# Splitting a whole 128x2048 weight unit per instruction in the expert stage, with three persistent places

## The chip, the cores and the metric

One Trainium2 chip, of which one core runs. The metric is device microseconds of one execution. Engines: TensorE (PE, with PEld for its weight loads), VectorE (DVE), ScalarE (ACT), GpSimd (POOL) and SyncE (SP), which issues the loads from HBM.

## The reference, cut to what matters

Three blocks on 256 tokens of width 1024: a hybrid layer, a retention block and a Fourier block with a mixture of experts. The change acts in the last part:

```
for e in range(N_EXPERTS):                       # 8 experts, top-k gates
    out = out + gates[:, e:e+1] * swiglu(t, w_gate[e], w_up[e], w_down[e])
```

where swiglu is (silu(t @ w_gate) * (t @ w_up)) @ w_down. Everything is float32.

## The kernel before, in words

All weights come as 475 **units** of 128x2048 float32 (1 MB). `fetch` (L101) starts one DMA on SP into a raw buffer; the raw buffers come from pools that grow as earlier tensors are released (6, then 4, 2 and 2 more), and a buffer that held an activation (xT) is used as one more in the experts, 15 in all there. A program-order list `raw` holds what has been fetched.

A float32 product is built from three fast products. `split` (L117) takes one **half** of the oldest raw unit, 128x1024: ScalarE copies it with rounding to wh (L128), VectorE writes the rest, raw - wh, to wl (L129). Both lie in a pool of WB = 4 halves. `half` (L171) issues the next split ahead and hands out the oldest split half. TensorE multiplies the activations' high part by wh, their low part by wh, and their high part by wl. So a split may write a place only when TensorE has read the half that was there, four halves earlier.

The experts start near 895 us: 8 experts of 42 units. An expert is 7 strips s = 0..6. A strip has 6 units, here called **G1, G2** (gate), **U1, U2** (up) and **D1, D2** (down, of strip s-1). The order is written out by hand for TensorE and SP only: G1, turn(s-1), G2, U1, U2, D1, D2. `turn` transposes h of the strip before (L1194 or L1196); ScalarE and VectorE then make hx from it (L1200, L1201), which the down units read. After the gate units ScalarE makes sg (L1177), after the up units VectorE makes h from the product and sg (L1184). The order on ScalarE and VectorE is set by a scheduler.

An expert with at most 64 tokens runs U and D **packed** (`either`): two matmuls (L1139, L1144) per piece in place of three (L1142, L1143, L1144), that is 8 matmuls per unit and not 12. Gate units always take 12. By their matmuls, experts 0, 2, 3, 4 are packed and 1, 5, 6, 7 are not. At an expert's end come y (L1232), at the start of the next one the sums into acc (L1254).

Of the kernel before, what the change touches and what calls it, by code (L numbers as in the profile page):

```python
# [9 lines left out]
F32 = mybir.dt.float32  # L10
F32R = mybir.dt.float32r
I32 = mybir.dt.int32
AF = mybir.ActivationFunctionType
ALU = mybir.AluOpType
AX = mybir.AxisListType

P = 128
# [5 lines left out]
E = 8  # L23
FE = 3584
NFE = FE // P
UN = 2048
UE = 42
# [36 lines left out]
def kernel(  # L64
# [10 lines left out]
    nc = tc.nc  # L75
    NU = ws_d.shape[0]
    WB = 4
    HP = 300
    HQ = 512
    HU = UN // 2  # L80

    NRAW, R2N, R3N, R4N = 6, 4, 2, 2
    const = ctx.enter_context(tc.tile_pool(name="const", bufs=1))
    rawp = ctx.enter_context(tc.tile_pool(name="rawp", bufs=NRAW))
    wp = ctx.enter_context(tc.tile_pool(name="wp", bufs=WB))
    psp = ctx.enter_context(tc.tile_pool(name="psp", bufs=2, space=bass.MemoryType.PSUM))
    ctx.enter_context(tc.manual_schedule(engines={mybir.EngineType.PE, mybir.EngineType.SP}))

# [1 line left out]
    raw = []  # L90
    wq = []
    nf = [0]

    def fetch(pool):

        if nf[0] < NU:
            t = pool if isinstance(pool, bass.AP) else pool.tile([P, UN], F32, tag="raw", name="raw")

            edges = {0: (0, HQ, HU, UN), NU - 1: (0, HU, UN)}.get(nf[0], (0, UN))
            for a, b in zip(edges, edges[1:]):  # L100
                nc.sync.dma_start(t[:, a:b], ws_d[nf[0]][:, a:b])  # L101
                if nf[0] == 0 and a < HU:
                    for k in (0,) if a == 0 else range(2, KD, 2):
                        nc.sync.dma_start(xT[:, k:k + 2], xT_d[:, k:k + 2])
            raw.append((t, pool))
            nf[0] += 1
        elif isinstance(pool, bass.AP):
            nc.sync.dma_start(pool[:, 0:D], fnorm_d)

    def more_room(name, n):  # L110
        pool = ctx.enter_context(tc.tile_pool(name=name, bufs=n))
        for _ in range(n):
            fetch(pool)

    half_ = [0, 0]

    def split(scales=None, between=None):  # L117


        if not raw or (half_[1] == H_F2 and scales is None):  # L120
            return
        half_[1] += 1
        r = raw[0][0][:, half_[0] * HU:(half_[0] + 1) * HU]
        wh = wp.tile([P, HU], F32R, tag="wh", name="wh")
        wl = wp.tile([P, HU], F32R, tag="wl", name="wl")
        if scales is None:
            for o in (slice(0, HQ), slice(HQ, HU)) if half_[1] == 1 else (slice(0, HU),):
                nc.scalar.activation(out=wh[:, o], in_=r[:, o], func=AF.Copy)  # L128
                nc.vector.tensor_tensor(out=wl[:, o], in0=r[:, o], in1=wh[:, o].bitcast(F32), op=ALU.subtract)  # L129
                if between is not None and o.start == 0:  # L130
                    between()
        else:
            for t in range(2):
                o = slice(t * 512, t * 512 + 512)
                nc.scalar.activation(out=wh[:, o], in_=r[:, o], func=AF.Copy, scale=scales[:, t:t + 1])
                nc.vector.scalar_tensor_tensor(out=wl[:, o], in0=r[:, o], scalar=scales[:, t:t + 1],
                                               in1=wh[:, o].bitcast(F32), op0=ALU.mult, op1=ALU.subtract)
        wq.append((wh, wl))
        if half_[0]:
            fetch(raw.pop(0)[1])  # L140
        half_[0] ^= 1
# [8 lines left out]
    def advance(item):  # L150
        try:
            item[0] = next(item[1]) or 1
        except StopIteration:
            side.remove(item)
# [16 lines left out]
    def half(ahead=True):  # L171

        for item in list(side):
            item[0] -= 1
            if item[0] <= 0:
                advance(item)
        if ahead:
            split()
        return wq.pop(0)

    def bank(tag="mm", shape=(P, 2, S)):
        return psp.tile(list(shape), F32, tag=tag, name=tag, bufs={"mm": 4, "sd": 2, "dn": 2}[tag])
# [3 lines left out]
    def mm3T(ps, u, b, xh, xl, start, stop):  # L186
        wh, wl = u
        c = slice(b * P, (b + 1) * P)
        mm(ps, wh[:, c], xh, start=start, stop=False)  # L189
        mm(ps, wh[:, c], xl, start=False, stop=False)  # L190
        mm(ps, wl[:, c], xh, start=False, stop=stop)  # L191
# [10 lines left out]
    def unit_late(xh, xl, late=2):  # L202

        ps = [bank("mm", (P, S)) for _ in range(2)]
        us = []
        for cb in range(2):
            us.append(half())
            for k in range(KD - late):
                mm3T(ps[cb], us[cb], k, xh[:, k], xl[:, k], k == 0, False)
        for cb in range(2):  # L210
            for k in range(KD - late, KD):
                mm3T(ps[cb], us[cb], k, xh[:, k], xl[:, k], False, k == KD - 1)
        return ps

    def stripX(xh, xl, mid=None):
# [51 lines left out]
    def col(c, n=1):  # L267
        return cols[:, c:c + n]
# [104 lines left out]
    with pa:  # L373
# [9 lines left out]
        def hilo(dst, j, src):  # L383
# [11 lines left out]
                                in1=col(C_N1, 8).unsqueeze(2).to_broadcast([P, KD, 4]), op=ALU.mult)  # L395
# [342 lines left out]
    with ExitStack() as pr:  # L738
# [120 lines left out]
        for c in range(KD):  # L859
            ps = bank("mm", (P, S))  # L860
            for j in range(16):
                if j % 8 == 0:
# [16 lines left out]
                            in1=col(C_FFN1, 8).unsqueeze(2).to_broadcast([P, KD, E]), op=ALU.mult)  # L879
# [4 lines left out]
    with ExitStack() as pn:  # L884
# [113 lines left out]
        with tc.high_priority(HP):  # L998
            for t in range(2):
# [3 lines left out]
                                    in1=L.unsqueeze(3).to_broadcast([P, 2, E, E]), op=ALU.subtract)  # L1003
# [7 lines left out]
        for c in range(0, KD, 2):  # L1011
            ps, o = to_tok(xT_, c, "mm")
# [8 lines left out]
        with tc.high_priority(HP):  # L1021
            nc.vector.scalar_tensor_tensor(out=pos.rearrange("p a b -> p (a b)"),
                                           in0=ps[:, 0:2].rearrange("p a b -> p (a b)"),
# [35 lines left out]


    pt.close()
    if R4N:
        more_room("raw4p", R4N)
    xT_flat = xT.rearrange("p a b -> p (a b)")
    fetch(xT_flat)
    fn = xT_flat[:, 0:D]
    with ExitStack() as pe:
# [214 lines left out]
        r = Q.tile([P, 2], F32, name="fr")  # L1282
# [12 lines left out]
        def out_rms():  # L1295
            nc.vector.tensor_tensor(out=v, in0=v4[:, :, 0], in1=v4[:, :, 1], op=ALU.add)
            rsqrt(r, v, 2, 1.0 / D)
# [6 lines left out]
        with tc.tile_pool(name="O", bufs=1) as O:  # L1304
            ecur = O.tile([P, E], F32, name="ecur")
            emask = O.tile([P, E], F32, name="emask")
            epos = O.tile([P, 2], F32, name="epos")
            egts = O.tile([P, 2], F32, name="egts")
            etmp = O.tile([P, 2, E], F32, name="etmp")
            with tc.If(n_over[0] + n_over[1] > 0):  # L1310

                nc.vector.tensor_copy(out=ecur, in_=io8)
                with tc.For_i(0, E, 1) as ev:
                    nc.vector.tensor_scalar(out=emask, in0=ecur, scalar1=-8.0, scalar2=None, op0=ALU.is_equal)
                    for src, dst in ((pos, epos), (gts, egts)):
                        nc.vector.tensor_tensor(out=etmp, in0=src, in1=emask.unsqueeze(1).to_broadcast([P, 2, E]), op=ALU.mult)
                        nc.vector.tensor_reduce(out=dst, in_=etmp, axis=AX.X, op=ALU.add)
                    nc.vector.tensor_scalar(out=epos, in0=epos, scalar1=float(-P), scalar2=None, op0=ALU.add)
                    cnt_ = [0]
                    cur_ = []  # L1320

                    def ohalf(ahead=True):
                        i, h = divmod(cnt_[0], 2)
                        if h == 0:
                            t = rawp.tile([P, UN], F32, tag="raw", name="oraw")
                            nc.sync.dma_start(t, ws_d[bass.ds(ev * UE + (NU - E * UE + i), 1)].rearrange("a p n -> p (a n)"))
                            cur_[:] = [t]
                        r = cur_[0][:, h * HU:(h + 1) * HU]
                        wh = wp.tile([P, HU], F32R, tag="wh", name="owh")
                        wl = wp.tile([P, HU], F32R, tag="wl", name="owl")  # L1330
                        nc.scalar.activation(out=wh, in_=r, func=AF.Copy)
                        nc.vector.tensor_tensor(out=wl, in0=r, in1=wh.bitcast(F32), op=ALU.subtract)
                        cnt_[0] += 1
                        return wh, wl

                    oex, osot, ors, steps = gather(lambda t: epos[:, t:t + 1], lambda t: epos[:, t:t + 1])
                    for f in steps:
                        f()
                    combine(experts(oex, ors, ohalf), osot, lambda t: egts[:, t:t + 1])
                    nc.vector.tensor_scalar(out=ecur, in0=ecur, scalar1=-1.0, scalar2=None, op0=ALU.add)  # L1340
                for hf in range(2):
                    out_sumsq(hf)
                out_rms()

        for hf in range(2):
            o = slice(hf * 512, hf * 512 + 512)
# [169 lines left out]
```

## Time and profile before

| what | us |
|---|---|
| runs: 1871.48, 1874.96, 1871.95; median | 1871.95 |
| the profiled execution, its own time | 1872.74 |
| its span | 1871.0 |
| PE busy | 1817.4 (97%) |
| DVE busy | 1482.0 (79%) |
| ACT busy | 1210.6 (65%) |
| L129 (wl), 906 instructions | 1078.5 |
| L128 (wh), 906 instructions | 922.0 |

The busy shares are averages over stages with different limits. In the expert stage VectorE is much busier than over the whole span, so the stage is read by windows and by its own rows.

### The profile page before, as it was taken

How to read it: one execution, taken by the hardware profiler on the slowest of the kernel's cores; microseconds unless marked ns; L12 is line 12 of the kernel's file. 1: busy time of each engine (PE TensorE's matmuls, PEld its weight loads, DVE VectorE, ACT ScalarE, POOL GpSimd, SP SyncE). 2: the span in 40 equal slices, each digit the busy share in tenths (PEclk: the TensorE clock that was granted, in tenths of full speed). 3: DMA queues.
4: the chain of work that ended last, by engine and by line, in shares of the span. 5: the costliest groups of instructions: out<-in, count | busy, mean ns of one | idle time of the engine just before them, and what ended most of it. 6: DMA issues, size and time to landing. Idle time of an engine off the chain costs nothing. (4 is left out here: it accounts for less than half of the span.)

```text
span 1871.0 us, 28740 instructions
## 1 busy us (share of the span) xinstructions
PE 1817.4 (97%) x10890; PEld 1574.5 (84%) x10890; DVE 1482.0 (79%) x1855; ACT 1210.6 (65%) x1484; POOL 158.2 (8%) x154
## 2 busy tenths in 40 slices
PE   8999999999999999999999999999999999999997
PEld 7999999999888999998777887777777788888885
DVE  5666676657677666656899989999999998988987
ACT  5765454455344444446787777888878777777775
POOL 2302122211111122110000000000000000000000
PEclk9999999999999999999999999999999999999999
DMA  8344544555444564544799998999999999999970
GB/s 313 140 154 168 193 178 183 181 181 197 158 150 159 189 248 184 187 170 180 295 419 377 353 367 326 411 386 377 415 354 413 381 353 364 332 356 354 343 290 36
DMA packets 71156, 505.77 MB, mean 270 GB/s; under 512 B 7888, under 2 KB 8016, under 8 KB 10320
## 3 DMA queue, kind: packets, MB, share of 16 engines
q1 hardware_dynamic: 70992, 503.53, 70.7%
q8 instruction: 110, 1.80, 0.4%
q14 instruction: 54, 0.44, 0.1%
HBM read 502.45 MB, written 1.05 MB: 269 GB/s over the span
## 5 line engine op out<-in xcount | busy, mean ns | idle before, releaser
L129 DVE TENSOR_TENSOR wl<-raw,wh 128x1024 fp32r<-128x1024 f32 (+1 forms) x906 | 1078.5, 1227 | 235.3 <-ACT wh L128 226.2
L128 ACT ACTIVATE wh<-raw 128x1024 fp32r<-128x1024 f32 (+1 forms) x906 | 922.0, 1053 | 428.9 <-PE mm L190 188.7
L189 PE MATMUL mm<-xh,wh 128*128 128x256 f32 x1248 | 357.5, 286 | 6.7 <-ACT xh L342 6.7
L1144 PE MATMUL mm<-wl,ex 128*128 128x512 f32 x896 | 356.0, 397 | 3.7 <-DVE wl L129 3.7
L190 PE MATMUL mm<-xl,wh 128*128 128x256 f32 x1248 | 355.2, 285 | 1.0 <-DVE xl L343 0.7
L191 PE MATMUL mm<-xh,wl 128*128 128x256 f32 x1248 | 354.9, 284 | 0.8 <-DVE wl L129 0.8
L1142 PE MATMUL mm<-wh,ex 128*128 128x512 f32 x672 | 270.4, 402 | 0.0
L1143 PE MATMUL mm<-wh,ex 128*128 128x512 f32 x672 | 266.1, 396 | 0.2 <-DVE ex L1103 0.2
L189 PEld LDWEIGHTS mm<-xh,wh 128*128 128x128 f32 x1248 | 237.9, 191 | 8.2 <-ACT xh L342 6.7
L190 PEld LDWEIGHTS mm<-xl,wh 128*128 128x128 f32 x1248 | 237.9, 191 | 2.4 <-DVE xl L343 2.3
L191 PEld LDWEIGHTS mm<-xh,wl 128*128 128x128 f32 x1248 | 237.7, 190 | 1.1 <-DVE wl L129 1.0
L1144 PEld LDWEIGHTS mm<-wl,ex 128*128 128x128 f32 x896 | 168.6, 188 | 54.2 <-DVE wl L129 13.7
L1144 PE MATMUL dn<-wl,hx 128*128 128x512 f32 x448 | 183.6, 410 | 12.1 <-DVE wl L129 11.9
L1143 PEld LDWEIGHTS mm<-wh,ex 128*128 128x128 f32 x672 | 126.7, 189 | 28.2 <-DVE ex L1103 0.5
L1142 PEld LDWEIGHTS mm<-wh,ex 128*128 128x128 f32 x672 | 126.6, 188 | 26.0 <-ACT wh L128 0.3
L1144 PEld LDWEIGHTS dn<-wl,hx 128*128 128x128 f32 x448 | 84.2, 188 | 55.8 <-DVE wl L129 40.1
L190 PE MATMUL mm<-hl,wh 128*128 128x256 f32 x352 | 99.8, 283 | 0.0
L191 PE MATMUL mm<-hh,wl 128*128 128x256 f32 x352 | 99.8, 283 | 0.0
L189 PE MATMUL mm<-hh,wh 128*128 128x256 f32 x352 | 99.8, 283 | 0.0
L1139 PE MATMUL dn<-wh,hx 128*128 128x512 f32 x224 | 89.2, 398 | 0.0
L1142 PE MATMUL dn<-wh,hx 128*128 128x512 f32 x224 | 88.9, 397 | 0.0
L1139 PE MATMUL mm<-wh,ex 128*128 128x512 f32 x224 | 88.7, 396 | 0.0
(400 smaller groups left out, 2500.7 us busy)
## 6 DMA issues: line engine op xcount, KB each, us to landing
raw<-in_ws_dram SPq DMA_DIRECT2D x451, 1024.0 KB, 6.3
xT<-in_ws_dram SPq DMA_DIRECT2D x22, 1024.0 KB, 7.0
raw<-in_ws_dram SPq DMA_DIRECT2D x3, 512.0 KB, 6.3
xT<-in_xT_dram SPq DMA_DIRECT2D x4, 256.0 KB, 5.4
xT<-in_xT_dram SPq DMA_DIRECT2D x1, 1024.0 KB, 8.3
out_dram<-acc SPq DMA_DIRECT2D x4, 256.0 KB, 2.1
cstA<-in_cst_dram SPq DMA_DIRECT2D x1, 576.0 KB, 9.1
raw<-in_ws_dram SPq DMA_DIRECT2D x2, 256.0 KB, 4.5
```

What stands on the lines that cost most here:

```text
L128: nc.scalar.activation(out=wh[:, o], in_=r[:, o], func=AF.Copy)
L129: nc.vector.tensor_tensor(out=wl[:, o], in0=r[:, o], in1=wh[:, o].bitcast(F32), op=ALU.subtract)
L189: mm(ps, wh[:, c], xh, start=start, stop=False)
L190: mm(ps, wh[:, c], xl, start=False, stop=False)
L191: mm(ps, wl[:, c], xh, start=False, stop=stop)
L1139: mm(out_, e, wh, start=first, stop=False)
L1142: mm(out_, e, wh, start=first, stop=False)
L1143: mm(out_, xk[:, P:2 * P], wh, start=False, stop=False)
L1144: mm(out_, e, wl, start=False, stop=last)
```

## The change

From the third expert unit on, one ScalarE and one VectorE instruction split a whole unit, 128x2048, at every second call of `split`. The four half places become two persistent tiles, `ring` (high and low parts, 4 halves each). In the experts the ring is seen as two places of a unit each; a third place, `wp3`, is added for high and low, and stands where two raw buffers (raw4p) were: 13 raw buffers are left in the experts. Units take the three places in turn, so a split waits for TensorE's last read of the unit three before: D1 for G2 of its own strip, D2 for U1, the next G1 for U2. The last unit is still split in halves.

```
-    NRAW, R2N, R3N, R4N = 6, 4, 2, 2
+    NRAW, R2N, R3N = 6, 4, 2
...
-    wp = ctx.enter_context(tc.tile_pool(name="wp", bufs=WB))
+    wp = ctx.enter_context(tc.tile_pool(name="wp", bufs=1))
+
+    ring = [wp.tile([P, WB, HU], F32R, name=f"ring{n}") for n in "hl"]
+    H_MOE = 2 * (NU - E * UE)
+    places = [[r.rearrange("p a n -> p (a n)")[:, i * UN:(i + 1) * UN] for r in ring] for i in (0, 1)]
+    if H_MOE % WB:
+        places.reverse()
...
+        if half_[1] >= H_MOE + WB:
+
+            r, pool = raw[0]
+            wide = half_[1] < 2 * NU - 2
+            if not (wide and half_[0]):
+                wh, wl = places[(half_[1] - H_MOE) // 2 % 3]
+                o = slice(0, UN) if wide else slice(half_[0] * HU, (half_[0] + 1) * HU)
+                nc.scalar.activation(out=wh[:, o], in_=r[:, o], func=AF.Copy)
+                nc.vector.tensor_tensor(out=wl[:, o], in0=r[:, o], in1=wh[:, o].bitcast(F32), op=ALU.subtract)
+                for i in range(2) if wide else half_[0:1]:
+                    wq.append((wh[:, i * HU:(i + 1) * HU], wl[:, i * HU:(i + 1) * HU]))
+                if wide or half_[0]:
+                    raw.pop(0)
+                    fetch(pool)
+            half_[0] ^= 1
+            half_[1] += 1
+            return
+        wh, wl = (r[:, half_[1] % WB] for r in ring)
...
-    if R4N:
-        more_room("raw4p", R4N)
+    wp3 = ctx.enter_context(tc.tile_pool(name="wp3", bufs=1))
+    places.append([wp3.tile([P, UN], F32R, name=f"place{n}") for n in "hl"])
```

ScalarE's order around the experts' steady strips, first before (expert 3, from one hx to the next; L1150 is the branch of a packed or unpacked piece):

```order
L1200 ACTIVATE hx<-sd 128x4x128
L128 ACTIVATE wh<-raw 128x1024
L1177 ACTIVATE sg<-mm,rsl 128x512
L128 ACTIVATE wh<-raw 128x1024
L1150 UNCONDITIONAL_BRANCH
L128 ACTIVATE wh<-raw 128x1024 x2
L1150 UNCONDITIONAL_BRANCH
L128 ACTIVATE wh<-raw 128x1024 x2
L1150 UNCONDITIONAL_BRANCH
L128 ACTIVATE wh<-raw 128x1024 x3
```

Now, in expert 0 from the third strip on, in all of expert 1 and in strips 2 and 3 of expert 2 (called **order A**): hx, D1 into the third place, sg, D2 into the ring. L1223 is hx, L1200 sg.

```order
L1223 ACTIVATE hx<-sd 128x4x128
L1173 UNCONDITIONAL_BRANCH
L135 ACTIVATE placeh<-xT 128x2048
L1200 ACTIVATE sg<-mm,rsl 128x512
L1173 UNCONDITIONAL_BRANCH
L135 ACTIVATE ringh<-raw 128x2048
```

And from strip 4 of expert 2 on (**order B**): hx, U2 into the ring, sg, and only then D1 into the third place.

```order
L1223 ACTIVATE hx<-sd 128x4x128
L135 ACTIVATE ringh<-raw 128x2048
L1173 UNCONDITIONAL_BRANCH
L1200 ACTIVATE sg<-mm,rsl 128x512
L135 ACTIVATE placeh<-raw 128x2048
```

So sg moved from between two halves to one whole unit before or behind D1's split. VectorE between an hx and the next h, before (expert 3):

```order
L1201 TENSOR_TENSOR hx<-sd,hx 128x4x128
L129 TENSOR_TENSOR wl<-xT,wh 128x1024
L129 TENSOR_TENSOR wl<-raw,wh 128x1024
L1150 UNCONDITIONAL_BRANCH
L129 TENSOR_TENSOR wl<-raw,wh 128x1024 x2
L1150 UNCONDITIONAL_BRANCH
L129 TENSOR_TENSOR wl<-raw,wh 128x1024
L1150 UNCONDITIONAL_BRANCH
L129 TENSOR_TENSOR wl<-raw,wh 128x1024
L1184 SCALAR_TENSOR_TENSOR h<-mm,rsl,sg 128x512
L129 TENSOR_TENSOR wl<-raw,wh 128x1024 x2
```

and now (expert 3, order B: hx, U2, D1, D2, h, G1):

```order
L1224 TENSOR_TENSOR hx<-sd,hx 128x4x128
L136 TENSOR_TENSOR ringl<-raw,ringh 128x2048
L1173 UNCONDITIONAL_BRANCH
L136 TENSOR_TENSOR placel<-raw,placeh 128x2048
L1173 UNCONDITIONAL_BRANCH
L136 TENSOR_TENSOR ringl<-xT,ringh 128x2048
L1207 SCALAR_TENSOR_TENSOR h<-mm,rsl,sg 128x512
L1173 UNCONDITIONAL_BRANCH
L136 TENSOR_TENSOR ringl<-raw,ringh 128x2048
```

Before, the second half of D2 followed h; now h stands behind all of D2, and the whole next G1 follows it.

## Rows read from the trace of the kernel before

**Rows 1.** The page, part 1: busy us, share of the span, instructions.

```profile
PE 1817.4 (97%) x10890; PEld 1574.5 (84%) x10890; DVE 1482.0 (79%) x1855; ACT 1210.6 (65%) x1484; POOL 158.2 (8%) x154
```

**Rows 2.** Windows, a packed and an unpacked one: us, busy by engine, PEclk, DMA share, GB/s.

```profile
1300.00:1350.00 50.00, 48.21 (x216) 36.81 (x216) 49.52 (x47) 42.05 (x47) 0.00 (x0) 1.00 1.01 416
1550.00:1600.00 50.00, 50.00 (x225) 40.43 (x225) 43.83 (x43) 37.67 (x43) 0.00 (x0) 1.00 0.96 355
```

**Rows 3.** Groups by form, 1265 to 1355 us: busy, mean ns, idle before.

```profile
L129 DVE TENSOR_TENSOR wl<-raw,wh 128x1024 fp32r<-128x1024 f32 x65 | 75.5, 1222 | 0.7
L128 ACT ACTIVATE wh<-raw 128x1024 fp32r<-128x1024 f32 x64 | 63.8, 1051 | 15.3 <-PE mm L1143 15.0 <-PE dn L1139 0.2
L1144 PE MATMUL dn<-wl,hx 128*128 128x512 f32 x43 | 18.7, 434 | 3.0 <-DVE wl L129 3.0
```

**Rows 4.** Timeline of VectorE in a packed strip: start, us.

```profile
1279.06 0.76 DVE L1184 SCALAR_TENSOR_TENSOR h<-mm,rsl,sg 128x512 f32<-128x512 f32 x1
1279.72 1.23 DVE L129 TENSOR_TENSOR wl<-xT,wh 128x1024 fp32r<-128x1024 f32 x1
...
1294.29 0.75 DVE L1184 SCALAR_TENSOR_TENSOR h<-mm,rsl,sg 128x512 f32<-128x512 f32 x1
1294.95 1.22 DVE L129 TENSOR_TENSOR wl<-raw,wh 128x1024 fp32r<-128x1024 f32 x1
```

**Rows 5.** Timeline of TensorE in the same strip.

```profile
1281.01 0.50 PE L1144 MATMUL dn<-wl,hx 128*128 128x512 f32 x1 [0.59 <-DVE wl L129]
...
1282.28 0.39 PE L1144 MATMUL mm<-wl,ex 128*128 128x512 f32 x1
...
1284.60 1.05 PE L1194 MATMUL sd<-cst,h 128*128 128x128 f32 x8
```

**Rows 6.** Timeline of ScalarE in the same strip.

```profile
1288.26 1.06 ACT L128 ACTIVATE wh<-raw 128x1024 fp32r<-128x1024 f32 x1 [0.34 <-PE mm L1143]
1289.22 0.67 ACT L1177 ACTIVATE sg<-mm,rsl 128x512 f32<-128x512 f32 x1
1289.79 6.73 ACT L128 ACTIVATE wh<-raw 128x1024 fp32r<-128x1024 f32 x7
```

**Rows 7.** Groups by form, 0 to 20 us: the only split pieces of another width.

```profile
L129 DVE TENSOR_TENSOR wl<-raw,wh 128x512 fp32r<-128x512 f32 x2 | 1.4, 692 | 3.1 <-ACT wh L128 3.1
...
L128 ACT ACTIVATE wh<-raw 128x512 fp32r<-128x512 f32 x2 | 1.2, 622 | 2.5 <-DMA raw<-in_ws_dram 2.5
```

**Rows 8.** Timeline of VectorE in an unpacked strip.

```profile
1650.50 0.75 DVE L1184 SCALAR_TENSOR_TENSOR h<-mm,rsl,sg 128x512 f32<-128x512 f32 x1
1651.16 4.62 DVE L129 TENSOR_TENSOR wl<-raw,wh 128x1024 fp32r<-128x1024 f32 x4
...
1656.57 1.23 DVE L129 TENSOR_TENSOR wl<-raw,wh 128x1024 fp32r<-128x1024 f32 x1 [0.79 <-ACT wh L128]
...
1662.02 5.77 DVE L129 TENSOR_TENSOR wl<-raw,wh 128x1024 fp32r<-128x1024 f32 x5 [1.35 <-ACT wh L128]
1667.70 0.75 DVE L1184 SCALAR_TENSOR_TENSOR h<-mm,rsl,sg 128x512 f32<-128x512 f32 x1
```

**Rows 9.** Timeline where an unpacked expert begins: VectorE, then TensorE.

```profile
1619.18 1.41 DVE L1254 SCALAR_TENSOR_TENSOR acc<-sd,gts,acc 128x512 f32<-128x512 f32 x2 [0.15 <-PE sd L1252]
1620.51 1.22 DVE L129 TENSOR_TENSOR wl<-raw,wh 128x1024 fp32r<-128x1024 f32 x1
1621.64 0.74 DVE L1184 SCALAR_TENSOR_TENSOR h<-mm,rsl,sg 128x512 f32<-128x512 f32 x1
...
1622.01 0.39 PE L1144 MATMUL mm<-wl,ex 128*128 128x512 f32 x1
1622.44 0.66 PE L1196 MATMUL sd<-cst,h 128*128 128x128 f32 x4
```

**Rows 10.** Timeline of SP's queue, and issue to landing of tile xT (min/median/max), 1230 to 1300 us.

```profile
1235.68 0.33 SPq L101 DMA_DIRECT2D xT<-in_ws_dram  x1
...
DMA to landing us min/median/max: 6.9/7.1/7.3
```

More of the change, by code (lines that the diff above doesn't have):

```diff
@@ L121, in split @@
             return
+        if half_[1] >= H_MOE + WB:
[15 more added lines that the diff above has]
+        wh, wl = (r[:, half_[1] % WB] for r in ring)
         half_[1] += 1
         r = raw[0][0][:, half_[0] * HU:(half_[0] + 1) * HU]
-        wh = wp.tile([P, HU], F32R, tag="wh", name="wh")
-        wl = wp.tile([P, HU], F32R, tag="wl", name="wl")
         if scales is None:
@@ L206, in unit_late @@
         for cb in range(2):
-            us.append(half())
+            us.append(half(ahead=not cb))
             for k in range(KD - late):
@@ L212, in unit_late @@
                 mm3T(ps[cb], us[cb], k, xh[:, k], xl[:, k], False, k == KD - 1)
+        split()
         return ps
@@ L1328, in ohalf @@
                         r = cur_[0][:, h * HU:(h + 1) * HU]
-                        wh = wp.tile([P, HU], F32R, tag="wh", name="owh")
-                        wl = wp.tile([P, HU], F32R, tag="wl", name="owl")
+                        wh, wl = (x[:, cnt_[0] % WB] for x in ring)
                         nc.scalar.activation(out=wh, in_=r, func=AF.Copy)
```

## The prediction

> **What bounds the kernel now.** I read the busy times first, then two windows of the expert stage, then single instructions. Over the span TensorE is busy 97% and VectorE only 79% [rows 1], which would say that splits are cheap. The windows say otherwise [rows 2]. In a packed stretch VectorE works 49.52 of 50 us and TensorE 48.21; in an unpacked one TensorE works all 50 and VectorE 43.83. So the eight experts have two limits: the four packed ones (0, 2, 3, 4) stand on VectorE and its coupling to TensorE, the four unpacked ones on TensorE alone. In 90 us around a packed strip VectorE idles only 0.7 us in front of its splits, TensorE waits 3.0 us in front of the down units for wl, and ScalarE waits 15 us, all of it for TensorE to release a place [rows 3]. A packed strip lasts 1294.29 - 1279.06 = 15.23 us from h to h [rows 4], an unpacked one 1667.70 - 1650.50 = 17.20 [rows 8].
>
> The packed strip is a loop through three engines, and it closes in rows. VectorE ends the second half of D2 at 1279.72 + 1.23 = 1280.95 [rows 4]; TensorE, which waited for it, goes on at 1281.01 and through the end of D2, G1, the turn and G2 [rows 5]. At 1288.26 TensorE's last reading of G2's wh releases ScalarE [rows 6]. ScalarE and VectorE work through U2's second half, sg, D1, half of D2 and h, and VectorE ends the second half of the next D2 at 1294.95 + 1.22 = 1296.17 [rows 4]. From end to end that is 15.22 us: 7.31 from VectorE's end to the release, 7.91 from the release to the next end. A strip gets shorter only if this loop does.
>
> **The change, part by part.**
>
> *Instructions.* 333 pairs of half splits become 333 whole ones. A VectorE split of 512 columns takes 692 ns, one of 1024 takes 1222 [rows 3, 7]: 530 ns per 512 columns, so a whole unit takes 1222 + 2 x 530 = 2282 ns (an estimate, like all that follows from it). Neighbours overlap: four halves take 4.62 us [rows 8], so the next starts (4.62 - 1.22) / 3 = 1.13 after the one before; at the same overlap of 0.09 a whole unit holds VectorE for 2.19 and not 2.27. That saves 0.07 to 0.08 us per unit, 0.45 per strip. On ScalarE 622 and 1051 ns give 429 per 512 columns, so 1.91 for a unit, and the next some 1.81 after its start. Whether VectorE's saving arrives is decided by the loop, since a consumer now waits for a whole unit: the first product with wl can't start after 1.22 us of VectorE, but after 2.28.
>
> *The places.* Four halves become six, but they are freed and filled in whole units. D1's split now waits for all of G2's wh to be read, which is the release at 1288.26; D2's waits for U1, the next G1's for U2.
>
> *The steady packed strip, order A* (sg behind D1). I start the clock at that release. ScalarE: D1 from 0, its next from 1.81; sg 1289.79 - 1289.22 = 0.57 [rows 6], to 2.38; D2 from 2.38 to 4.29. Its place, U1's, is free by then: eight matmuls at the pitch of 0.233 (ten from 1282.28 to 1284.60 are 2.32 [rows 5]) are 1.9 us. VectorE: D2 from 4.32, h from 6.51 for 1294.95 - 1294.29 = 0.66 [rows 4], G1 from 7.17 to 9.45. D2 now lies whole ahead of h, and G1, the unit whose wl TensorE wants next, lies behind it. TensorE goes on 0.06 later, at 9.51. From G1's first product with wl to the release rows give 1288.26 - 1282.28 = 5.98 [rows 5, 6]. Sum 15.49: **+0.28** against 15.21. TensorE's work in the strip is no cover for it; TensorE now waits ahead of G1 instead of D2.
>
> *Order B* (sg ahead of D1). sg needs G2's two last products, 2 x 0.233 after the release's matmul, which I count as 0.23 past the release; then 0.57: D1 starts at 0.80 on ScalarE and ends at 2.71. D2 follows from 2.61 to 4.52. VectorE: D1 from 2.74 to 4.93 (D1 is the later one now, since VectorE has nothing ready ahead of it), D2 to 7.12, h to 7.78, G1 to 10.06; TensorE from 10.12; release at 16.10: **+0.89**.
>
> *Count.* From the second h of an expert on there are five steady strips. Order A: five in expert 0, two in expert 2, 7 x 0.28 = 2.0. Order B: three in expert 2, five each in experts 3 and 4, 13 x 0.89 = 11.6. Together +13.6 us. The two unknowns in it are the length of a whole-unit split, bounded by twice a half (2.45 with nothing saved, which would add 0.17 or 0.34 per strip) and by 2 x 1.13, and whether the orders hold.
>
> *The first strips of the four packed experts.* They have no down units, but the same step: a consumer one whole unit behind. No row shows it alone; nearest is order A's +0.28 and at most one more half, 1.13. I take 0.4 each, 1.6 in all, with 0 to 4.5 as bounds.
>
> *Expert 0, first packed strips.* ScalarE and VectorE split U2 of strip 1 ahead of U1, while TensorE uses U1 first. At worst that puts one whole unit, 2.19, in front; at best TensorE is late anyway, 0. I take 1.5, since at this place VectorE is nearer to being full than to being idle [rows 2].
>
> *The starts of unpacked experts.* Between acc and h stands one half, 1.13 us, and the turn starts 0.06 us after h's end (1621.64 + 0.74 = 1622.38 against 1622.44 [rows 9]). There a whole unit stands now: 2.19 - 1.13 = 1.06 more, and TensorE, which never idles here, has nothing to put in front. The unit ahead of it also comes behind the pair of acc at twice the grain: between 0 and the pair's 1.33 us [rows 9], I take 0.5, the lower part, since the turn's wait covers what precedes it. Four times 1.5 is 6.2. The steady unpacked strips I cost at nothing: VectorE idles 0.79 + 1.35 = 2.14 us in each [rows 8], and orders A and B add at most 0.89 to a loop that has this slack. If that cover fails, each of 20 strips loses up to 0.9.
>
> *Raw buffers.* Two fewer of 15. A load into xT is issued at 1235.68 and lands 7.1 us later (at most 7.3) [rows 10], and VectorE splits the unit's second half at 1279.72 [rows 4]: over 35 us of lead. A strip of six units per 15.2 us makes one unit 2.5 us, so two buffers take off 5 us. Cost nothing; its cover would go only if transfers came 30 us later.
>
> *Stages before the experts* keep their halves; the ring has the same four places. Nothing, at most 1 us.
>
> Sum: 13.6 + 1.6 + 1.5 + 6.2 = +22.9. The profiled execution took 1872.74, which is 0.8 above the median of 1871.95: 1895.6 against it, **1895** against the median.
>
> The trace shows VectorE nearly saturated in packed experts [rows 2], with ScalarE and TensorE waiting [rows 3]. The Trainium skill, "Perfetto Trace Analysis", section Optimizing Scalar/DVE Operations, has a rule for each side: "Grouping and performing larger operations can improve throughput if the engine is saturated", and, where an engine isn't saturated but makes bubbles elsewhere, breaking instructions up may let work be completed sooner. By the first rule the change saves (first rival); by the second it costs (the forecast). In this trace VectorE is both, 99% busy and the cause of TensorE's waits, so neither rule decides; the loop does.
>
> **The rivals.**
>
> *VectorE sets the packed strip (faster).* If the loop has slack that I don't see, each unit saves 0.075 us where VectorE is the limit: four packed experts of 42 units, 168 x 0.075 = 12.6 us, 1859. For it: 0.7 us of idle time in 90 [rows 3]. Against it: TensorE's 3.0 us of waits there and a loop that closes to 0.01 us. It decides if the loop of order A is under 14.8 us, that is, if I have 0.7 too much in it: a finer release, or h and G1 in another order. Chance 0.14. It is what the first of the two rules of the Trainium skill above would give.
>
> *No change.* Order A's loop comes to 15.2, order B's lead is taken up by the two extra half places, and the starts lose what the strips gain: within 3.7 us of 1872. For it: six places and not four. Against it: both orders fix what lies in front of G1 on VectorE. Chance 0.11.
>
> *Unpacked strips lose as well.* TensorE's reading of U1 takes 12 matmuls there and not 8, 0.9 us more before D2 can be split, and the idle 2.14 us is used up. 20 strips x 0.6 = 12 more: 1907. Chance 0.09.
>
> *Loads too late*: with over 30 us of lead, below 0.02, within the slower side.
>
> **How the numbers follow.** The forecast has 0.65, and a range of its own of 1884 to 1906: unpacked starts at 0 or at 2.4 each, packed strips at A's price or with no saving in the split. A measurement here can tell about 0.2%, 3.7 us, from no change. Faster by more 0.14, within it 0.11, slower 0.75 (0.65 + 0.09 + 0.01). The range runs from 1868, the low edge of no change, to 1908, which takes in the unpacked rival; outside lie the faster rival and the tail above, together about 0.2.
>
> **What would show it.** In the new profile: splits of 2.28 us on VectorE and 1.91 on ScalarE; h to h 15.5 in order A and 16.1 in order B, with TensorE waiting for wl in front of G1 and VectorE idle 1 us or more per packed strip; 17.20 unchanged in unpacked strips; a wait of about 1 us ahead of the turn at the starts of unpacked experts. A packed strip under 15.2, or VectorE without idle time there, proves the loop wrong. Waits for a DMA in ScalarE's splits would mean that the raw buffers matter.

## The result, and the profile after

The changed kernel takes 1898.1 us (median of 4 runs, 1897.4 to 1900.2) against 1871.7 for the kernel before: ratio 1.0141, 95% interval 1.0123 to 1.0158. It is 26 us slower, 3 us from the predicted 1895. The profiled execution took 1898.17 with a span of 1896.4; before it was 1871.0, so 25.4 us are to be found in the two traces.

The page, part 1, and two groups of part 5 of the changed kernel (L136 is VectorE's whole split, L135 ScalarE's):

```profile
PE 1815.7 (96%) x10890; PEld 1574.3 (83%) x10890; DVE 1462.0 (77%) x1522; ACT 1180.4 (62%) x1151; POOL 158.1 (8%) x154
...
L136 DVE TENSOR_TENSOR ringl<-raw,ringh 128x2048 fp32r<-128x2048 f32 x205 | 468.0, 2286 | 47.7 <-ACT ringh L135 46.8
...
L135 ACT ACTIVATE ringh<-raw 128x2048 fp32r<-128x2048 f32 x205 | 389.9, 1912 | 85.3 <-PE mm L1166 56.7
```

(Two labels ahead of the prediction are off. ScalarE's order before, with sg between two halves, is one of the unpacked expert 5 and not of expert 3; VectorE's order now, with D2 from xT, stands in experts 2 and 4 and not in 3. In the packed experts before, sg stands behind both halves of U2 and ahead of D1, as [rows 6] show; so order B leaves it there, and order A moves it one unit back. No number of the forecast rests on these labels.)

The change did what it says: VectorE is 20 us less busy and ScalarE 30 us less than in [rows 1], with 333 instructions fewer on each. A whole split takes 2286 ns on VectorE (2282 were worked out) and 1912 on ScalarE (1909). The kernel is slower because less work is now done in each packed microsecond. The same two windows as [rows 2], a packed and an unpacked one:

```profile
1300.00:1350.00 50.00, 46.14 (x200) 34.26 (x198) 45.30 (x25) 38.38 (x26) 0.00 (x0) 1.00 0.98 391
1550.00:1600.00 50.00, 50.00 (x223) 40.44 (x222) 43.22 (x24) 37.07 (x24) 0.00 (x0) 1.00 0.97 365
```

In the packed one VectorE fell from 49.52 to 45.30 us and TensorE from 48.21 to 46.14, at an unchanged clock: each now waits for the other, VectorE by way of ScalarE's half of the split. The groups by form of expert 3's packed strips (1290 to 1371 us) say where TensorE waits, in front of G1 (ringl) and of D1 (placel):

```profile
L1167 PE MATMUL mm<-ringl,ex 128*128 128x512 f32 x60 | 24.7, 412 | 2.5 <-DVE ringl L136 2.5
...
L1167 PE MATMUL dn<-placel,hx 128*128 128x512 f32 x21 | 8.7, 417 | 2.9 <-DVE placel L136 2.9
```

A strip of order A, in expert 0: ScalarE first (D1, sg, then D2 and G1), then VectorE from one h to the next (only the rows that the loop goes through).

```profile
967.40 1.93 ACT L135 ACTIVATE placeh<-xT 128x2048 fp32r<-128x2048 f32 x1 [1.25 <-PE mm L1166]
969.22 0.67 ACT L1200 ACTIVATE sg<-mm,rsl 128x512 f32<-128x512 f32 x1
969.79 3.71 ACT L135 ACTIVATE ringh<-raw 128x2048 fp32r<-128x2048 f32 x2
```

```profile
958.35 0.75 DVE L1207 SCALAR_TENSOR_TENSOR h<-mm,rsl,sg 128x512 f32<-128x512 f32 x1
...
971.73 2.29 DVE L136 TENSOR_TENSOR ringl<-raw,ringh 128x2048 fp32r<-128x2048 f32 x1
973.94 0.74 DVE L1207 SCALAR_TENSOR_TENSOR h<-mm,rsl,sg 128x512 f32<-128x512 f32 x1
974.60 2.28 DVE L136 TENSOR_TENSOR ringl<-raw,ringh 128x2048 fp32r<-128x2048 f32 x1
```

TensorE's last reading of the place that D1 takes releases ScalarE at 967.40. From there the rows give sg at 1.82, D2 on ScalarE at 2.39, D2 on VectorE at 4.33, h at 6.54, G1 at 7.20: the prediction had 1.81, 2.38, 4.32, 6.51 and 7.17. From h to h it is 973.94 - 958.35 = 15.59. TensorE takes up G1's first product with wl at 976.94, 0.06 after the end of VectorE's G1, and ScalarE's next release comes at 982.99, 6.05 later:

```profile
976.94 0.50 PE L1167 MATMUL mm<-ringl,ex 128*128 128x512 f32 x1 [0.50 <-DVE ringl L136]
```

```profile
982.99 1.91 ACT L135 ACTIVATE placeh<-raw 128x2048 fp32r<-128x2048 f32 x1 [1.25 <-PE mm L1166]
```

A strip of order B, in expert 3, in the same way:

```profile
1299.58 0.69 ACT L1200 ACTIVATE sg<-mm,rsl 128x512 f32<-128x512 f32 x1 [0.35 <-PE mm L1167]
1300.16 1.91 ACT L135 ACTIVATE placeh<-raw 128x2048 fp32r<-128x2048 f32 x1
1301.98 3.70 ACT L135 ACTIVATE ringh<-raw 128x2048 fp32r<-128x2048 f32 x2
```

```profile
1290.30 0.74 DVE L1207 SCALAR_TENSOR_TENSOR h<-mm,rsl,sg 128x512 f32<-128x512 f32 x1
...
1302.11 2.29 DVE L136 TENSOR_TENSOR placel<-raw,placeh 128x2048 fp32r<-128x2048 f32 x1 [0.56 <-ACT placeh L135]
1304.31 2.28 DVE L136 TENSOR_TENSOR ringl<-raw,ringh 128x2048 fp32r<-128x2048 f32 x1
1306.52 0.75 DVE L1207 SCALAR_TENSOR_TENSOR h<-mm,rsl,sg 128x512 f32<-128x512 f32 x1
```

sg waits 0.35 for G2's last product, D1 stands behind it, and VectorE waits 0.56 for D1: 1306.52 - 1290.30 = 16.22. An unpacked strip of the changed kernel (VectorE's h in expert 5) lasts 1597.26 - 1580.10 = 17.16, against 17.20 in [rows 8]:

```profile
1580.10 0.74 DVE L1207 SCALAR_TENSOR_TENSOR h<-mm,rsl,sg 128x512 f32<-128x512 f32 x1
...
1597.26 0.74 DVE L1207 SCALAR_TENSOR_TENSOR h<-mm,rsl,sg 128x512 f32<-128x512 f32 x1
```

And the start of the unpacked expert 6, VectorE and then TensorE, which answers to [rows 9]:

```profile
1640.90 1.41 DVE L1277 SCALAR_TENSOR_TENSOR acc<-sd,gts,acc 128x512 f32<-128x512 f32 x2 [0.94 <-PE sd L1275]
1642.23 2.28 DVE L136 TENSOR_TENSOR placel<-raw,placeh 128x2048 fp32r<-128x2048 f32 x1
1644.43 0.74 DVE L1207 SCALAR_TENSOR_TENSOR h<-mm,rsl,sg 128x512 f32<-128x512 f32 x1
```

```profile
1645.23 0.66 PE L1219 MATMUL sd<-cst,h 128*128 128x128 f32 x4 [1.10 <-DVE h L1207]
```

The turn now waits 1.10 us for h behind a whole unit.

Taking every h of both traces, the 25.4 us come from these places:

| where | predicted | measured |
|---|---|---|
| 7 steady packed strips, order A | +2.0 | +2.5 |
| 13 steady packed strips, order B | +11.6 | +12.8 |
| first strips of packed experts, and the swap in expert 0 | +3.1 | +3.5 |
| unpacked experts, from the last h of the expert before to their last h | +6.2 | +3.4 |
| start of expert 2 (+1.8), of 3 and 4 (-0.4 each) | 0 | +1.1 |
| the end, behind the last h | 0 | +2.0 |

Of the 3.5, 0.6 is the later first h of expert 0. It is the least certain number here, as executions differ ahead of it: one ScalarE instruction of the first stage, shown at experiment 8, starts 1.7 us later in the changed kernel's trace (50.68) than in the one before (48.95), though the work up to there is the same in both.

### The profile page after: what moved, and what is told of

It reads as the page before. It is cut to its first block, busy times and chain, and to the rows that moved or that the text cites. A ratio compares the mean times of both kernels' runs of the same rounds, so it can differ in the third digit from the quotient of the medians.

```text
span 1896.4 us, 27661 instructions
## 1 busy us (share of the span) xinstructions
PE 1815.7 (96%) x10890; PEld 1574.3 (83%) x10890; DVE 1462.0 (77%) x1522; ACT 1180.4 (62%) x1151; POOL 158.1 (8%) x154
## 5 line engine op out<-in xcount | busy, mean ns | idle before, releaser
L136 DVE TENSOR_TENSOR ringl<-raw,ringh 128x2048 fp32r<-128x2048 f32 x205 | 468.0, 2286 | 47.7 <-ACT ringh L135 46.8
L151 DVE TENSOR_TENSOR ringl<-raw,ringh 128x1024 fp32r<-128x1024 f32 (+1 forms) x282 | 349.0, 1239 | 180.2 <-ACT ringh L150 174.8
L150 ACT ACTIVATE ringh<-raw 128x1024 fp32r<-128x1024 f32 (+1 forms) x282 | 295.8, 1052 | 288.3 <-PE mm L212 190.6
L135 ACT ACTIVATE ringh<-raw 128x2048 fp32r<-128x2048 f32 x205 | 389.9, 1912 | 85.3 <-PE mm L1166 56.7
L211 PE MATMUL mm<-xh,ringh 128*128 128x256 f32 x1248 | 355.8, 285 | 7.2 <-ACT xh L365 7.2
L212 PE MATMUL mm<-xl,ringh 128*128 128x256 f32 x1248 | 353.6, 283 | 1.0 <-DVE xl L366 0.7
L213 PE MATMUL mm<-xh,ringl 128*128 128x256 f32 x1248 | 353.2, 283 | 1.4 <-DVE ringl L151 1.4
L1167 PE MATMUL mm<-ringl,ex 128*128 128x512 f32 x672 | 269.5, 401 | 15.0 <-DVE ringl L136 15.0
L136 DVE TENSOR_TENSOR placel<-raw,placeh 128x2048 fp32r<-128x2048 f32 (+1 forms) x105 | 238.1, 2269 | 39.3 <-ACT placeh L135 30.9
L135 ACT ACTIVATE placeh<-raw 128x2048 fp32r<-128x2048 f32 (+1 forms) x105 | 199.5, 1900 | 41.5 <-PE mm L1166 18.8
L1166 PE MATMUL mm<-ringh,ex 128*128 128x512 f32 x464 | 183.1, 395 | 0.2 <-DVE ex L1126 0.2
L1165 PE MATMUL mm<-ringh,ex 128*128 128x512 f32 x464 | 183.1, 395 | 0.0
```

Of the source, the lines that this page charges most:

```text
L1165: mm(out_, e, wh, start=first, stop=False)
L1166: mm(out_, xk[:, P:2 * P], wh, start=False, stop=False)
L1167: mm(out_, e, wl, start=False, stop=last)
```

## The experiments

The theory was that whole units close a loop through three places: TensorE releases G2's place, ScalarE splits D1, makes sg, splits D2, VectorE splits D2, makes h, splits all of G1, and only then can TensorE go on. Rivals: the scheduler's new order, the two raw buffers, or the whole unit as such, whatever the places.

Experiments 1 to 7 and 9 to 12 have ScalarE's order written out by hand in the experts, so that a part of the change can be put back without the scheduler moving others: 1 to 7 for the experts as a whole, by the first line below, 9 to 12 only inside the strips, by the line that experiment 9 shows in its place. The edit, in the changed kernel (cut):

```
+        pe.enter_context(tc.manual_schedule(engines={..., mybir.EngineType.Activation}))
...
-                nc.scalar.activation(out=sg[s], in_=ps, func=AF.Silu, scale=rs)
+                return lambda: nc.scalar.activation(out=sg[s], in_=ps, func=AF.Silu, scale=rs)
```

The closure is called behind the split of D1. hx is put off in the same way: in experiments 1 to 4 behind U1's split, from 5 on behind U2's.

**1. Order A everywhere, three places, whole units.**

> The changed kernel with one thing fixed by hand in the experts: ScalarE's order is written out, sg behind D1's split in every strip (order A everywhere). Theory (a loop from TensorE's release of G2's place over ScalarE's D1, sg, D2 and VectorE's D2, h, G1 back to TensorE): every steady packed strip takes 15.58 us, as the order A strips of the changed kernel do, none 16.2; unpacked strips stay 17.17; 13 strips x 0.62 = 8 us less, about 1890. Rival (the scheduler's new order alone is the loss, not the whole unit): packed strips go back to 15.2 and the time to about 1880 or less. Rival (long instructions or fewer raw buffers): strips of order A and B keep 15.6 and 16.2 wherever they stand, no change.

Every steady packed strip took 15.55 to 15.59 us, as the theory said, and the unpacked ones 17.17. The time was 1908.9, ratio 1.0176 (1.0156 to 1.0195), not 1890: the borders between experts, in the hand-made order, came 20 us longer in sum than in the changed kernel. And the strips were right for two reasons at once, which experiments 4 and 5 showed.

**2. Halves in the three places.** In addition:

```
-            wide = half_[1] < 2 * NU - 2
+            wide = False
```

> As e1, with three persistent places and 13 raw buffers kept, but every unit split in two halves on ScalarE and VectorE. Theory (the whole unit is what costs): six half places open the loop, VectorE's work alone is the limit, 12 x 1.135 + 0.66 + 0.60 = 14.88 us, so packed strips of 14.9 to 15.0, below the 15.21 of before; time about 1867. Rival (two raw buffers fewer): strips stay at 15.6 or above, waits for DMA show in front of splits, about 1890. Rival (persistent places in themselves): the same 1890 without DMA waits.

Most packed strips took 14.88 to 15.05, one 15.49; where single ones are shorter (13.74 to 13.85, one 12.61), h stands one or two halves earlier in VectorE's order. 1872.1 us, ratio 0.9988 (0.9977 to 1.0000): above the expected 1867, with borders 9 us longer in sum than before, and 37 us below experiment 1, which has the same places, buffers and hand-made order. So neither the persistent places nor the buffers are what costs.

**3. Whole units on ScalarE alone.**

```
-                nc.vector.tensor_tensor(out=wl[:, o], in0=r[:, o], in1=wh[:, o].bitcast(F32), op=ALU.subtract)
+                for q in (slice(0, HU), slice(HU, UN)) if wide else (o,):
+                    nc.vector.tensor_tensor(out=wl[:, q], in0=r[:, q], in1=wh[:, q].bitcast(F32), op=ALU.subtract)
```

> As e1, but only ScalarE splits whole units; VectorE takes them in two halves, and TensorE can go on after the first. Theory: what costs is VectorE's whole unit in front of TensorE; G1's first half is there 1.06 us earlier, the loop falls to 14.5 and VectorE's work (14.88) is the limit: packed strips 14.9 to 15.0, about 1867. Rival (ScalarE's whole unit, which holds the place and sg, costs as much): strips of 15.5, about 1890.

VectorE's h in expert 3 (rows between left out): 1326.26 - 1311.38 = 14.88.

```profile
1311.38 0.75 DVE L1214 SCALAR_TENSOR_TENSOR h<-mm,rsl,sg 128x512 f32<-128x512 f32 x1
...
1326.26 0.74 DVE L1214 SCALAR_TENSOR_TENSOR h<-mm,rsl,sg 128x512 f32<-128x512 f32 x1
```

It is VectorE's work and no more: the window shows it busy for all 50 us.

```profile
1300.00:1350.00 50.00, 48.22 (x221) 38.05 (x220) 50.00 (x48) 40.06 (x27) 0.00 (x0) 1.00 1.01 421
```

In experts 2 to 4 one strip each takes 13.74, with h a half earlier, as in 2. 1875.2 us, ratio 1.0008 (0.9995 to 1.0021). The loss of the steady strips hangs on VectorE's whole unit in front of TensorE; ScalarE's costs nothing there.

**4. Four places.** The fourth takes the space of two more raw buffers, from the Fourier stage on:

```
-    if R3N:
-        more_room("raw3p", R3N)
+    wp4 = ctx.enter_context(tc.tile_pool(name="wp4", bufs=1))
+    place4 = [wp4.tile([P, UN], F32R, name=f"fourth{n}") for n in "hl"]
...
-                wh, wl = places[(half_[1] - H_MOE) // 2 % 3]
+                wh, wl = places[(half_[1] - H_MOE) // 2 % 4]
```

> As e1, whole units on both engines, but four places of a unit in place of three, and two raw buffers fewer again (11). Theory: a split then waits for the unit four before, D1 for G1 and not G2, so the loop is open and the saving of whole units arrives: VectorE's 6 x 2.193 + 1.26 = 14.42 us is the limit, packed strips 14.4 to 14.5, about 1858, faster than before. Rival (whole units cost in themselves, by the later first product): strips stay near 15.6, about 1890. Rival (raw buffers matter): ScalarE waits for DMA and TensorE's idle time grows in all strips, over 1900.

A miss: strips of 15.53 to 15.57 and 1908.9 us, as in experiment 1. Taken alone it would speak for the rival. ScalarE's and VectorE's timelines in a packed strip show another path:

```profile
1317.73 0.60 ACT L1233 ACTIVATE hx<-sd 128x512 fp32r<-128x512 f32 x1 [3.57 <-PE sd L1224]
```

```profile
1320.16 2.29 DVE L136 TENSOR_TENSOR ringl<-raw,ringh 128x2048 fp32r<-128x2048 f32 x1 [0.99 <-ACT ringh L135]
```

ScalarE no longer waits for a place. It waits 3.57 us for the turn, with U2's split behind hx, and VectorE then waits for U2. The path turn, hx, U2, D1, D2, h, G1, turn happens to be as long as the loop over G2's place. So experiment 1 had both, and couldn't tell them apart.

**5. Experiment 1 with hx behind U2's split.**

> As e1, but hx stands behind U2's split on ScalarE, as in the order A strips of the changed kernel, since in e1 ScalarE sat in front of hx until the turn was done and VectorE then waited for U2. Theory (the loop over G2's place is the limit): packed strips stay at 15.57, and the waits of ScalarE in front of D1 are for TensorE's last reading of G2. Rival (in e1 it was the path turn, hx, U2, D1, D2, h, G1): that path is open now, strips fall to VectorE's 14.4.

```profile
1319.05 1.92 ACT L135 ACTIVATE placeh<-raw 128x2048 fp32r<-128x2048 f32 x1 [1.25 <-PE mm L1168]
1320.88 0.67 ACT L1204 ACTIVATE sg<-mm,rsl 128x512 f32<-128x512 f32 x1
```

```profile
1310.01 0.74 DVE L1212 SCALAR_TENSOR_TENSOR h<-mm,rsl,sg 128x512 f32<-128x512 f32 x1
...
1325.59 0.75 DVE L1212 SCALAR_TENSOR_TENSOR h<-mm,rsl,sg 128x512 f32<-128x512 f32 x1
```

Still 15.58 (1325.59 - 1310.01), and now D1 waits for TensorE's reading of wh by gate matmuls (L1168). The time is 1909.4 (two runs), ratio 1.0203 (1.0182 to 1.0223). With the path over hx open, the loop over the place holds the strip by itself.

**6. Experiment 4 with hx behind U2's split.** Here, and in 7, y also stands behind the splits of G2 and U1 at the borders.

> As e4 (whole units, four places, 11 raw buffers), with hx behind U2's split on ScalarE and, at the experts' borders, y behind the splits of G2 and U1. Theory: in e4 the place's wait was gone and the path turn, hx, U2, D1, D2, h, G1 held the strip at 15.57 instead; with both open VectorE's work is the limit: packed strips 14.42 to 14.5, 20 x 0.75 = 15 us less than before in them, 1856 to 1862 in all. Rival (a whole unit costs by its later first product, whatever the places): 15.5 again, about 1890. Rival (11 raw buffers are too few): strips above 15 with waits of ScalarE for DMA.

Strips of 14.47 in all four packed experts (one in each is shorter, as in 2): the loop is open, and whole units then do give their saving. The borders came out far worse, with 7 to 11 us of idle time on VectorE in most of them. I put that down to my order, which has each gathering step on ScalarE in front of a whole split; that step isn't shown by itself, but with the borders left to the scheduler (experiment 9) most of the loss is gone. 1896.2 us, ratio 1.0127 (1.0110 to 1.0144).

**7. Experiment 3 with the same two moves.**

> As e3 (whole units on ScalarE only, halves on VectorE, three places), with hx behind U2's split and y behind the splits of G2 and U1 at the borders. Theory: strips at VectorE's work of 14.88 as in e3, borders 1.5 to 3 us shorter than in e3 (7 of them), so about 1862 to 1866. Rival: the borders of e3 lose for another reason than ScalarE's order of y, and the time stays at 1875.

Strips of 14.88 again (one shorter in each packed expert from 2 on). The borders were 1 to 4 us longer than in experiment 3 instead of shorter: 1895.0 us, ratio 1.0125 (1.0108 to 1.0142). The move of hx alone had left the borders as they were (5 against 1, within 0.1 us), so the move of y is what cost; the strips don't depend on it.

**8. The kernel before with two raw buffers fewer.**

```
-    NRAW, R2N, R3N, R4N = 6, 4, 2, 2
+    NRAW, R2N, R3N, R4N = 6, 4, 2, 0
```

> The kernel before with two raw buffers fewer in the experts (13) and nothing else. Theory (loads have over 30 us of lead): no change, 1872 within 2 us, strips of 15.21 and 17.20. Rival (raw buffers matter): above 1878, with waits for DMA in front of splits.

A miss: 1878.8 us, ratio 1.0034 (1.0021 to 1.0046). But no split in the experts waits for a DMA, and strips of 15.22 and 17.20 are as before except for four in expert 4, three of them of 16.77. ScalarE in one of these:

```profile
1449.67 1.05 ACT L128 ACTIVATE wh<-raw 128x1024 fp32r<-128x1024 f32 x1
1451.98 0.69 ACT L1177 ACTIVATE sg<-mm,rsl 128x512 f32<-128x512 f32 x1 [1.26 <-PE mm L1144]
1452.57 7.68 ACT L128 ACTIVATE wh<-raw 128x1024 fp32r<-128x1024 f32 x8
```

Fewer buffers made the scheduler put sg ahead of both halves of U2 in these strips, where it waits for G2's last product and the halves behind it wait along; in [rows 6] sg stands behind the half that the release lets go. It is the mechanism of order B, at half the grain. That is 5 us. The other 2 of this trace are there 49 us after its start, long before the fourth pool of raw buffers exists, and at this place the traces differ anyhow. ScalarE's same table load in the kernel before, here, and in experiment 9 (another line number, the same instruction):

```profile
48.95 1.28 ACT L422 ACT_TABLE_LOAD   x1
```

```profile
50.77 1.28 ACT L422 ACT_TABLE_LOAD   x1
```

```profile
48.04 1.28 ACT L445 ACT_TABLE_LOAD   x1
```

So they say nothing of the buffers, and 5 us lies within the interval.

**9. Four places, whole units, the borders left to the scheduler.** The hand-made order of 5 and 6 (without the moves of y) is kept only inside the strips:

```
+            with tc.manual_schedule(engines={..., mybir.EngineType.Activation}):
+                for s in range(1, 7):
+                    silu = gate_strip(s, lambda: turn(s - 1))
+                    up_strip(s, silu)
+                    if s < 6:
+                        down(s - 1)
+            down(5, lambda: turn(6))
```

> Whole units on both engines, four places, 11 raw buffers; ScalarE's order by hand (hx behind U2, sg behind D1) only from strip 1 to the up units of strip 6, the experts' borders left to the scheduler, since the hand-made order of e6 lost 5 us and more at each border. Theory: steady packed strips 14.47 as in e6 (20 x 0.74 = 15 us less than before), borders about 1.7 us longer than before at the unpacked starts as in the changed kernel, so 1856 to 1866, faster than before. Rival (the borders lose by the whole unit or the fewer raw buffers, not by the order): they stay over 30 us from the last h of an expert to the first of the next, and the time stays above 1885.

1864.9 us, ratio 0.9951 (0.9937 to 0.9965): faster than before. Its packed window shows VectorE full, and its h rows 14.47:

```profile
1300.00:1350.00 50.00, 49.01 (x229) 39.57 (x228) 50.00 (x28) 40.45 (x28) 0.00 (x0) 1.00 1.01 420
```

```profile
1304.12 0.75 DVE L1212 SCALAR_TENSOR_TENSOR h<-mm,rsl,sg 128x512 f32<-128x512 f32 x1
...
1318.59 0.75 DVE L1212 SCALAR_TENSOR_TENSOR h<-mm,rsl,sg 128x512 f32<-128x512 f32 x1
```

**10. Whole units on ScalarE alone, three places, borders as in 9.**

> Whole units on ScalarE only, halves on VectorE, three places, 13 raw buffers, with the same order as e9. Theory: steady packed strips 14.88 (20 x 0.33 = 6.6 us less than before), borders within 1 us of before since VectorE keeps its halves there: 1864 to 1870. Rival (borders lose with ScalarE's whole unit too): 1875 and more, as in e3.

1862.9 us, ratio 0.9941 (0.9927 to 0.9954), the fastest median. h to h 14.88 (one strip of 13.74 in each of experts 2 to 4):

```profile
1321.02 0.75 DVE L1212 SCALAR_TENSOR_TENSOR h<-mm,rsl,sg 128x512 f32<-128x512 f32 x1
...
1335.90 0.75 DVE L1212 SCALAR_TENSOR_TENSOR h<-mm,rsl,sg 128x512 f32<-128x512 f32 x1
```

**11. Halves, three places, borders as in 9.**

> Halves on both engines, three places, 13 raw buffers, with the same order as e9. Theory: packed strips 14.9 to 15.0 and borders as before: 1863 to 1869; the gap to e9 is what whole units are worth once the loop is open (0.41 per packed strip), less what they cost at the borders. Rival (raw buffers or persistent places cost at the borders): above 1872.

1865.6 us, ratio 0.9956 (0.9943 to 0.9970), strips of 14.88. Experiments 9, 10 and 11 lie within 3 us of each other and their intervals overlap. In open strips whole units win 0.41 us each on VectorE (9 against 11), some 8 us in 20 strips; most of it is lost where experts begin. By the traces, 9 has the first h of expert 0 3 us later than 11, and takes some 3 us more in sum from the last h of one expert to the first of the next; the medians are 0.7 apart. From the last h of expert 5 to the third of expert 6 it takes 58.2 us in 9, 57.0 in 10 and 11, and 57.1 before.

**12. Three places, whole units, borders as in 9.** The changed kernel, but for the order in the strips.

> The changed kernel (whole units on both engines, three places, 13 raw buffers) with the same order as e9 to e11. Theory: the order is worth 13 strips x 0.62 = 8 us, the rest of the loss stays, since three whole places close the loop: packed strips 15.57 in all four packed experts, time 1888 to 1893; together with e9 (a fourth place), e10 and e11 (halves in front of TensorE) the same order is then faster than before only where the loop is open. Rival (the scheduler's order was the loss and three places are no limit): 1872 or less.

1891.7 us, ratio 1.0098 (1.0081 to 1.0115). The same order that is 8 to 11 us faster than before in 9, 10 and 11 is 18 us slower here:

```profile
1321.95 0.75 DVE L1211 SCALAR_TENSOR_TENSOR h<-mm,rsl,sg 128x512 f32<-128x512 f32 x1
...
1337.52 0.75 DVE L1211 SCALAR_TENSOR_TENSOR h<-mm,rsl,sg 128x512 f32<-128x512 f32 x1
```

15.57 from h to h. So of the changed kernel's 26 us, 6 to 8 are the scheduler's order (6 from 1898.1 to 1891.7, 8 when each is held against its own runs of the kernel before; the trace has 13 strips by 0.62, less some 2 elsewhere). The rest is the whole unit on VectorE in only three places, with its borders, but for the 2 us at the end, whose cause is open.

## Why the prediction was right, point by point

- *What bounds the kernel.* Right. The steady packed strips carry some 15 of the 25.4 us, though VectorE became 20 us less busy over the span.
- *The instructions.* 2282 against 2286 ns on VectorE, 1.91 against 1.912 us on ScalarE.
- *Order A.* 15.49 was predicted, 15.58 measured; order B 16.10 and 16.21. Every step up to G1's split agreed within 0.03 us. What was short is the last piece, from G1's first product with wl to the release: 5.98 by [rows 5, 6], 6.05 measured (976.94 to 982.99). Against the loop of 15.22 this left 0.28 and 0.89 where 0.36 and 0.99 came. Two signs were not quite met: in order A TensorE still waits 0.24 us ahead of D2 (at 974.08), in order B 0.58 per strip ahead of D1 (2.9 in five strips), and not only ahead of G1; and in order A VectorE's wait for D1 is 0.77 us (at 969.36), where 1 or more was named.
- *That the loop is the limit and not the grain as such.* Shown by 9 against 12 (a fourth place opens it), by 10 and 11 (halves in front of TensorE open it), and by 5, which excludes the path over hx.
- *First strips and the swap in expert 0.* 3.1 predicted, 3.5 measured; the share of the swap isn't shown by itself.
- *Starts of unpacked experts.* The mechanism is there (the turn waits 1.10 us; 1.06 was predicted), but "four times 1.5" is wrong in its parts: experts 1, 6 and 7 start 1.8 us later and expert 5 only 0.1, 5.4 in all. The steady unpacked strips, put at nothing, gave back 2.6, most of it in one strip in each of experts 5, 6 and 7 that took 17.89 us before and now takes 17.17. With the first strips (+0.6) the net is 3.4 for 6.2.
- *Not foreseen:* the same start at expert 2, which is packed (+1.8), and the end (+2.0). The late start seems to go with the expert before: 2, 6 and 7 follow an unpacked expert, 3, 4 and 5, which lost next to nothing, a packed one. Expert 1 is the exception, and no run settles it.
- *The sum.* That 1895 came within 3 us is partly luck: the terms for the packed experts were 2.1 us short in sum, the one for the unpacked experts 2.8 too high, and 3.1 us came at places that the sum doesn't have.
- *Raw buffers at no cost.* Right as far as loads go. In the changed kernel two of ScalarE's splits do wait for a load, 0.45 us at 960.18 and 0.28 at 1340.79, which the prediction had as a sign that buffers matter; but the strips there last 15.59 and 16.20 like their neighbours. In experiment 8 two buffers fewer cost 5 us all the same, by way of the scheduler's order in one expert; the step "cost nothing" named only transfers as the thing that could go wrong.
- *The rivals.* VectorE's saving exists: 14.88 becomes 14.47 in 6 and 9, where the loop is open. The point given for it, a loop under 14.8, was not met by the changed kernel. Unpacked strips did not lose: 17.17 in all of them.
- *Of the two rules of the Trainium skill* ("Perfetto Trace Analysis", Optimizing Scalar/DVE Operations) both hold here, by the loop: grouping on VectorE gave 0.41 us per strip with four places, and breaking up gave 15.57 - 14.88 = 0.69 with three.

## What to carry to other kernels

Before instructions are made larger, write down the loop from the release of a buffer to its next release, with the larger instruction in each place where someone waits for all of it; the saving of overhead arrives only if that loop stays below the engine's own work. Larger pieces want more places: 15.57 with three whole units, 14.47 with four, while halves in the space of three units reach 14.88. Over the whole kernel the size of the pieces was then worth little: 1864.9 with whole units in four places, 1865.6 with halves, both in the same hand-made order. And an instruction that waits late, such as sg here, stops all that stands behind it in its engine's order, so its place in the order is worth as much as the size of the pieces (0.62 us in 13 strips).

## What was not expected of the hardware

Behind the last expert VectorE's sequencer passes the branch over the block for overflowing tokens, which isn't taken in either kernel. The waits view around it, in the kernel before and in the changed one:

```profile
DVE acc L1348 <- DVEq L1310: 1.8, 1, 1.8
```

```profile
DVE acc L1370 <- DVEq L1333: 4.1, 1, 4.1
```

It took 4.1 to 4.4 us in all eleven experiments built on the changed kernel, also with halves, and 1.8 in the one built on the kernel before. That is 2.3 of the 26 us, at a place where the work is the same; what of the change causes it stays open.
